# Streams' new states from rows that lie twice, high and low parts in turn, one stream per quarter of 32 rows

## The chip, the cores and the metric

The kernel runs on one core of a Trainium2 chip. The time is the device time of one execution of the whole program, in microseconds (us), and the measure of a kernel is the median of its runs. One further execution was taken with the hardware profiler; its trace gives every instruction's start and end.

## The reference

One layer of a hybrid encoder trunk in float32, for a prompt of 256 frames and for 8 running streams of 16 frames each (384 tokens in all). What matters here is the state space branch (SSD). For each of 8 groups with 8 heads of 64 channels, a new state is computed from the projected and convolved x and B:

```python
step(h, chunk):
    cum = cumsum(dt * A);  xdt = x * dt
    w_end = exp(cum[last] - cum)
    h = h * exp(cum[last]) + einsum('bsgn,bsgr,bsgrp->bgrpn', B, w_end, xdt)
```

The prompt's state starts at zero. Each of the 8 streams starts at its own state and has one chunk of 16 frames, so its new state is the old one decayed plus a sum over its 16 rows of B (128 wide) times the weighted x (64 channels by head). This sum, for 8 streams at once, is what the change rewrites.

## The kernel before

Work is done in stages: early projections and the pooling branch, then the SSD stage (about 420 to 1165 us of the span), then the gate, the output projections and the MLP. TensorE (PE) works through all of them almost without a pause, on products of three: each float32 operand is split into a high part (fp32r) and a low rest, and high times high, high times low and low times high are added up.

A weight block of 128x1024 comes by DMA (`w`), ScalarE (ACT) copies it to its high part (`wh`, line 70) and VectorE (DVE) subtracts for the low part (`wl`, line 71). `take` holds up to three split blocks ahead of PE. A half projection uses one block in 24 matmuls (`half`), and a projection is two halves.

**The SSD stage** loops over 8 groups g. A group has ten projections: x0, B, x1, C, x2, then x3, z0, z1, z2, z3. Two pairs of 128-channel tiles are made of x0..x3: pair 0 (j = 0, 1) and pair 1 (j = 2, 3). Between projections stand two "lumps" of short matmuls: the first after x2, the second after z3. The first lump of a group finishes pair 1 of the group before, the second one pair 0 of the same group. A lump holds t_pp (prompt's state, line 710), in the first lump t_cb (line 666, `cb`), then t_yT and t_Y (lines 688 and 696, `Y`), t_yi (line 675, `py`) and t_su (line 808, `su`). Code written as `lump(...)` is issued in this order on PE.

**t_su** is the sum above. The rows of the streams lie as 128 partitions, 16 for each stream. A matmul contracts 32 rows, a quarter of the array, which are two streams. `Bm` is B times a 0/1 mask that keeps one of the two streams, `xhl` the weighted x in high and low part. For two streams of a quarter, three products and four quarters there are 24 matmuls of 256 columns, into four PSUM tiles `su`. Then DVE adds them to the states (`hs`, line 817).

The pool of PSUM tiles named `ss` has six buffers, given out in turn. In a first lump `cb`, two `Y` and four `su` are seven. So the fourth `su` takes the buffer of `cb`, and its first matmul waits until DVE has read `cb` (`mside`, line 745, which writes `cbm`).

**How x gets its rows.** `turned` makes three steps, run by `tick` at successive half projections: DVE transposes blocks of 32 (`xb`, line 626), POOL issues four DMAs to a DRAM scratch (`t_scr`, line 631), POOL issues one DMA back (line 637), into `xT` (two tiles j of three blocks of 128 rows: two of the prompt, one of the streams) or for B into `Bt`. `xside` (line 761) multiplies by dt for `xdt` and by the weights in place, `hside` (lines 770 and 771) splits into `xhl`, `bside` (lines 723 to 727) splits B and makes `Bm`. All of POOL's DMAs stand in one order on POOL, with its additions of `ssum`.

The order of instructions on each engine is set when the program is built: a scheduler follows the code's order and puts an instruction earlier where it takes its operands to be ready. On the chip each engine runs its own list in that order.

Of the kernel before, what the change touches and what calls it, by code (L numbers as in the profile page):

```python
# [14 lines left out]
P = 128  # L15
T = 384
TP = 256
NB = 8
TS_ = 16
# [3 lines left out]
NH = 64  # L23
# [7 lines left out]
V_GPRE, V_GMLP, V_PSC, V_CW, V_CB, V_NRM, V_DSK, V_DTB, V_ALOG, V_PAR, V_END = 0, 16, 32, 48, 240, 288, 320, 352, 353, 354, 384  # L31


def build(ctx, tc, io):
    nc = tc.nc
    v, s, te, gp, sy = nc.vector, nc.scalar, nc.tensor, nc.gpsimd, nc.sync
# [5 lines left out]
    dram = ctx.enter_context(tc.tile_pool(name="dram", bufs=1, space=DRAM))  # L42
# [3 lines left out]
    vec = consts.tile([P, V_END], F32, name="vec")  # L46
# [6 lines left out]
    def sstile(name):  # L53
        return pss.tile([P, 512], F32, tag="ss", name=name)
# [19 lines left out]
    def dve_later():  # L74
        return behind(cut[1])
# [53 lines left out]
    steps = []  # L129
# [80 lines left out]
    ma_scr = [dram.tile([P, T], F32, name=f"ma_scr{i}") for i in range(KD)]  # L210
    gb_scr = [dram.tile([P, T], F32, name=f"gb_scr{i}") for i in range(KD)]
    t_scr = [dram.tile([T, P], F32, name=f"t_scr{i}") for i in range(40)]
    cum_scr = dram.tile([NH, T], F32, name="cum_scr")
    dec_scr = dram.tile([NH, NB], F32, name="dec_scr")

# [69 lines left out]
    turn, low = [None], [None]  # L285
# [65 lines left out]
    for b in range(3):  # L351
# [3 lines left out]
            out=dgl[:, b, :], in0=ident, scalar=y1, in1=dgh[:, b, :].bitcast(F32), op0=ALU.mult, op1=ALU.subtract  # L355
# [217 lines left out]
    with tc.tile_pool(name="phd", bufs=2, reuse_waits="tile") as pd, tc.tile_pool(  # L573
        name="phd1", bufs=1, reuse_waits="tile"
# [4 lines left out]
        for i in range(3):  # L579
            b = pd1.tile([P, 24, 19], F32, name=f"cbuf{i}")  # L580
# [37 lines left out]
        def conv(ui, c, tag, nb):  # L618
            return taps(conv_in(ui, c), c, tag, nb)

        def turned(src, i, o):
            xb, scr = [], t_scr[i]

            def turn():
                xb.append(pd.tile([P, T], F32, tag="xb", name=f"xb{i}"))
                v.transpose(xb[0], src)

            def spread():
                for q in range(4):
                    p32 = slice(q * 32, q * 32 + 32)  # L630
                    gp.dma_start(
                        scr[:, p32].rearrange("(j a) b -> a j b", a=32),
                        xb[0][p32].rearrange("p (j b) -> p j b", b=32),
                    )

            wait = [lambda: None] if i < 32 else []
            steps.append(wait + [turn, spread, lambda: gp.dma_start(o, scr.rearrange("(b t) n -> t b n", b=3))])

        def xturned(D, g, j):
            S = D.p[j // 2]  # L640
            if j % 2 == 0:
                S.xT = pd.tile([P, 2, 3, P], F32, tag="xT", name=f"xT{S.nm}", bufs=1)
            turned(D.xs[j], g * 4 + j, S.xT[:, j % 2])

        def lump(fn):
            with behind(last[0]):
                last[0] = fn()
# [70 lines left out]
            return i  # L718

        def bside(D):  # L720
            D.Bhl = pd.tile([P, 2, 3, P], F32R, tag="Bhl", name=f"Bhl{D.g}", bufs=1)
            with dve_later():
                s.activation(D.Bhl[:, 0], D.Bt, AF.Copy)
                v.tensor_tensor(D.Bhl[:, 1], D.Bt, D.Bhl[:, 0].bitcast(F32), ALU.subtract)
            D.Bm = pd.tile([P, 2, 2, P], F32R, tag="Bm", name=f"Bm{D.g}", bufs=1)
            for h in range(2):
                s.activation(
                    D.Bm[:, h],
                    D.Bhl[:, :, 2, :].bitcast(F32),
                    AF.Copy,  # L730
                    scale=vec[:, V_PAR + h : V_PAR + h + 1],
                )

        def cside(D):
# [21 lines left out]
        def xside(S):  # L756
            S.xdt = pd.tile([P, 2, 3, P], F32, tag="xdt", name=f"xdt{S.nm}", bufs=1)
            for q in range(2):
                tv = S.xT[:, q].rearrange("p b (h q) -> p b h q", h=2)
                for o, i in ((S.xdt, 3), (S.xT, 6)):  # L760
                    v.tensor_tensor(
                        o[:, q].rearrange("p b (h q) -> p b h q", h=2),
                        tv,
                        tok[:, i : i + 3, S.h0 + q * 2 : S.h0 + q * 2 + 2].unsqueeze(3).to_broadcast([P, 3, 2, 64]),
                        ALU.mult,
                    )

        def hside(S):
            S.xhl = pd.tile([P, 2, 2, 3, P], F32R, tag="xhl", name=f"xhl{S.nm}", bufs=1)
            S.split = s.activation(S.xhl[:, 0], S.xT, AF.Copy)  # L770
            v.tensor_tensor(S.xhl[:, 1], S.xT, S.xhl[:, 0].bitcast(F32), ALU.subtract)

        def eside(S, q):
            if q == 0:
# [26 lines left out]
        def state(S):  # L801
            def t_su():
                su = [sstile(f"su{S.nm}_{q}") for q in range(4)]
                for h in range(2):
                    for n, (bl, xl) in enumerate(((0, 0), (0, 1), (1, 0))):
                        for q in range(4):
                            t = slice(q * 32, q * 32 + 32)
                            i = te.matmul(
                                pairs(su[q][:, h * 256 : h * 256 + 256]),
                                S.D.Bm[t, h, bl, :],  # L810
                                S.xhl[t, xl, :, 2, :].rearrange("p j n -> p n j"),
                                start=n == 0,
                                stop=n == 2,
                            )
                for q in range(4):
                    hr = S.hs[:, 2 * q : 2 * q + 2].rearrange("p h (a n) -> p h a n", a=2)
                    v.tensor_tensor(hr, hr, su[q].rearrange("p (h n a) -> p h a n", h=2, a=2), ALU.add)
                return i

            lump(t_su)  # L820
            gp.dma_start(io["new_ssm_s"][S.qd], S.hs)
# [52 lines left out]
        for g in range(G + 1):  # L874
            if g == G:
                S = prev.p[1]
# [29 lines left out]
            D = Pair()  # L906
# [11 lines left out]
            D.Bt = pd.tile([P, 3, P], F32, tag="Bt", name=f"Bt{g}", bufs=1)  # L918
            turned(D.BT, 32 + g, D.Bt)
# [16 lines left out]
            S = D.p[0]  # L936
# [36 lines left out]
            with nullcontext() if g else behind(S.split):  # L973
                bside(D)
# [24 lines left out]
    with ExitStack() as phe:  # L999
# [21 lines left out]
        for i in range(KD):  # L1021
# [4 lines left out]
            h = mp.tile([P, T], F32R, name=f"mh{i}")  # L1026
            l = mp.tile([P, T], F32R, name=f"ml{i}")
# [42 lines left out]
    with tc.tile_pool(name="phf", bufs=1, side="right", reuse_waits="tile") as pf, tc.tile_pool(  # L1070
        name="phf2", bufs=2, side="right", reuse_waits="tile"
# [79 lines left out]
        for nb in range(4):  # L1151
# [3 lines left out]
            o = [sstile(f"wo{nb}_{b}") for b in range(3)]  # L1155
# [138 lines left out]
        with behind(cd[0]):  # L1294
            for b in range(3):
# [3 lines left out]
                    out=dgl[:, b, :], in0=ident, scalar=y, in1=dgh[:, b, :].bitcast(F32), op0=ALU.mult, op1=ALU.subtract  # L1299
# [12 lines left out]
    with tc.tile_pool(name="phg", bufs=1, reuse_waits="tile") as pg, tc.tile_pool(  # L1312
        name="phg2", bufs=2, reuse_waits="tile"
# [8 lines left out]
        for c8 in range(NC):  # L1322
            hh = []
            for f8 in range(8):
                f = c8 * 8 + f8
                ps = ups[f] if f < 3 else proj([io["w_up"][f, 0], io["w_up"][f, 1]], xs2, f"up{f}")
                t = pg2.tile([P, T], F32, tag="t", name=f"ht{f}")
                for c, w in ((slice(0, TP), slice(0, P)), (slice(TP, T), slice(P, 192))):
                    v.scalar_tensor_tensor(
                        out=halves(t[:, c]), in0=even_odd(ps)[:, :, w], scalar=0.0, in1=halves(r2[:, c]), op0=ALU.max, op1=ALU.mult  # L1330
                    )
                s.activation(t, t, AF.Square)
                h = pg2.tile([P, T], F32R, tag=f"hh{f8}", name=f"hh{f}", bufs=1)
                l = pg2.tile([P, T], F32R, tag=f"hl{f8}", name=f"hl{f}", bufs=1)
# [3 lines left out]
            for nb in range(4):  # L1338
                o = [sstile(f"wd{c8}_{nb}_{b}") for b in range(3)]
# [168 lines left out]
```

## Time and profile before

| | |
|---|---|
| median of 3 runs | 2644.0 us (2642.28 to 2645.38) |
| profiled execution, its own time | 2643.02 us |
| its span, first to last instruction | 2641.2 us |
| around the span | 1.8 us |
| mean granted clock of PE | 0.999 |
| busy: PE, DVE, ACT, POOL | 2629.5, 1545.1, 1162.2, 240.9 us |
| the stretch 594 to 683 us (one group): PE, DVE, ACT, POOL busy | 89.00, 76.30, 56.07, 24.48 us |

A row of a timeline gives the start in us from the span's start, the duration, the engine, the source line, the operation with output and inputs, the shape and how many; in brackets stands how long the engine sat idle before it and what ended that. A duration on PE overlaps the next one, so the spacing of starts tells what a matmul costs; the chain of waits gives these pieces without overlap.

### The profile page before, as it was taken

To read this page: it belongs to the slowest core of one execution; us is meant where nothing else is said; L and a number is where in the kernel's file an instruction comes from. 1 tells how busy PE (TensorE), PEld (TensorE's weight loads), DVE (VectorE), ACT (ScalarE), POOL (GpSimd) and SP (SyncE) were. 2 spreads that over 40 slices of the span, in tenths; PEclk is the share of its full clock that TensorE was granted. 3 is DMA by queue.
4 is the path that set the end of the run, shared out by engine and by line. 5 is a ranking of instruction groups with operands and counts; after the bars stand their busy time and mean duration, and the time that the engine had idled before them with its cause. 6 is when DMAs were issued, how large, how long until landed. Compare 5 with 4: busy or idle time off the path is not lost.

```text
span 2641.2 us, 40719 instructions
## 1 busy us (share of the span) xinstructions
PE 2629.5 (100%) x16317; PEld 2527.7 (96%) x16317; DVE 1545.1 (58%) x2192; ACT 1162.2 (44%) x1781; POOL 240.9 (9%) x382
## 2 busy tenths in 40 slices
PE   9999999999999999999999999999999999999998
PEld 9999999999999999999999989999999999989897
DVE  6685335788888888867444336534444444444446
ACT  6443224656565756545333336433333333323233
POOL 0000002122222322211000000000000000000000
PEclk9999999999999999999999999999999999999999
DMA  7444446666666666657555543444444444444443
GB/s 276 153 132 159 148 145 213 194 203 226 216 228 201 222 219 235 218 190 261 163 166 160 195 149 132 144 136 136 136 136 136 136 136 136 135 135 136 134 135 132
DMA packets 130318, 451.50 MB, mean 171 GB/s; under 512 B 17936, under 2 KB 24912, under 8 KB 125136
## 3 DMA queue, kind: packets, MB, share of 16 engines
q1 hardware_dynamic: 103552, 361.44, 42.3%
q0 software_dynamic: 19520, 72.64, 7.7%
q10 hardware_dynamic: 7056, 14.81, 1.8%
q8 instruction: 128, 2.10, 0.3%
q14 instruction: 62, 0.51, 0.1%
HBM read 404.49 MB, written 44.34 MB: 170 GB/s over the span
## 4 chain that ended last, share of the span: by engine, by line
PE 97%; DMA 1%; DVE 1%; issue 1%; ACT 1%; SPq 0%; DVEq 0%; POOL 0%; ACTq 0%; POOLq 0%
PE pj_up L101 6%; PE pj_up L102 6%; PE pj_up L103 6%; PE wd L156 6%; PE wd L154 6%; PE wd L155 6%; PE pj_x L101 5%; PE pj_x L103 4%; PE pj_x L102 4%; PE pj_sp L103 3%; PE pj_sp L101 3%; PE pj_sp L102 3%; PE pj_z L103 3%; PE pj_z L102 3%; PE pj_z L101 3%; PE pj_gb L101 2%
## 5 line engine op out<-in xcount | busy, mean ns | idle before, releaser
L101 PE MATMUL pj_up<-x1h,wh_up 128*128 128x384 f32 (+1 forms) x1024 | 333.7, 326 | 0.0
L102 PE MATMUL pj_up<-x1l,wh_up 128*128 128x384 f32 (+1 forms) x1024 | 333.4, 326 | 0.0
L103 PE MATMUL pj_up<-x1h,wl_up 128*128 128x384 f32 (+1 forms) x1024 | 333.4, 326 | 0.0
L71 DVE TENSOR_TENSOR wl_wd<-w_wd,wh_wd 128x1024 fp32r<-128x1024 f32 x126 | 154.3, 1225 | 240.3 <-ACT wh_wd L70 240.3
L154 PE MATMUL wd<-wh_wd,hh 128*128 128x512 f32 x756 | 286.5, 379 | 0.0
L155 PE MATMUL wd<-wl_wd,hh 128*128 128x512 f32 x756 | 286.5, 379 | 0.0
L156 PE MATMUL wd<-wh_wd,hl 128*128 128x512 f32 x756 | 286.5, 379 | 0.0
L70 ACT ACTIVATE wh_wd<-w_wd 128x1024 fp32r<-128x1024 f32 x126 | 133.1, 1057 | 321.6 <-PE wd L156 261.2
L70 ACT ACTIVATE wh_up<-w_up 128x1024 fp32r<-128x1024 f32 x126 | 133.1, 1057 | 292.0 <-PE pj_up L102 231.8
L71 DVE TENSOR_TENSOR wl_up<-w_up,wh_up 128x1024 fp32r<-128x1024 f32 x126 | 154.3, 1225 | 178.0 <-ACT wh_up L70 178.0
L101 PE MATMUL pj_x<-xgh,wh_x 128*128 128x384 f32 x768 | 252.0, 328 | 0.3 <-ACT wh_x L70 0.3
L103 PE MATMUL pj_x<-xgh,wl_x 128*128 128x384 f32 x768 | 250.5, 326 | 0.7 <-DVE wl_x L71 0.7
L102 PE MATMUL pj_x<-xgl,wh_x 128*128 128x384 f32 x768 | 250.4, 326 | 0.0
L102 PEld LDWEIGHTS pj_up<-x1l,wh_up 128*128 128x128 f32 x1024 | 193.6, 189 | 0.2
L101 PEld LDWEIGHTS pj_up<-x1h,wh_up 128*128 128x128 f32 x1024 | 193.6, 189 | 0.2
L103 PEld LDWEIGHTS pj_up<-x1h,wl_up 128*128 128x128 f32 x1024 | 193.6, 189 | 0.0
L103 PE MATMUL pj_z<-xgh,wl_z 128*128 128x384 f32 x512 | 167.2, 327 | 0.0
L101 PE MATMUL pj_z<-xgh,wh_z 128*128 128x384 f32 x512 | 166.9, 326 | 0.0
L102 PE MATMUL pj_z<-xgl,wh_z 128*128 128x384 f32 x512 | 166.9, 326 | 0.0
L101 PE MATMUL pj_sp<-abh,wh_sp 128*128 128x384 f32 x512 | 166.9, 326 | 0.0
L102 PE MATMUL pj_sp<-abl,wh_sp 128*128 128x384 f32 x512 | 166.9, 326 | 0.0
L103 PE MATMUL pj_sp<-abh,wl_sp 128*128 128x384 f32 x512 | 166.9, 326 | 0.0
(334 smaller groups left out, 6177.0 us busy)
## 6 DMA issues: line engine op xcount, KB each, us to landing
w_up<-w_up SPq DMA_DIRECT2D x128, 512.0 KB, 3.5
w_wd<-w_down SPq DMA_DIRECT2D x128, 512.0 KB, 3.5
w_x<-w_in SPq DMA_DIRECT2D x96, 512.0 KB, 4.0
w_z<-w_in SPq DMA_DIRECT2D x64, 512.0 KB, 4.4
w_sp<-w_ssd SPq DMA_DIRECT2D x64, 512.0 KB, 3.5
w_ga<-w_ga SPq DMA_DIRECT2D x32, 512.0 KB, 3.5
w_pp<-w_pp SPq DMA_DIRECT2D x32, 512.0 KB, 3.5
hs<-ssm POOLq DMA_DIRECT2D x16, 1024.0 KB, 7.8
```

Of the source, the lines that this page charges most:

```text
L70: cut[0] = s.activation(h, w, AF.Copy)
L71: cut[1] = v.tensor_tensor(l, w, h.bitcast(F32), ALU.subtract)
L101: te.matmul(out, wh, xh, start=first, stop=False, **how)
L102: te.matmul(out, wh, xl, start=False, stop=False, **how)
L103: return te.matmul(out, wl, xh, start=False, stop=last, **how)
L154: te.matmul(out, mh, vh, start=k == 0 and b != held, stop=False, skip_group_check=b == held)
L155: te.matmul(out, mh, vl, start=False, stop=False, skip_group_check=b == held)
L156: last[0] = te.matmul(out, ml, vh, start=False, stop=k == nk - 1, skip_group_check=b == held)
```

## The change

The streams' rows come twice. A new helper `doubled` issues two more DMAs for each tile, one to the even and one to the odd partitions: partitions 2t and 2t+1 both hold row t of the first four streams (l = 0) and of the last four (l = 1). So a quarter of 32 partitions holds one stream of 16 rows, twice, and a second one in the other half of the free dimension. The new tile for x is `xD`, for B `BD`, and the weights come the same way into `tokd`, once, by way of a DRAM scratch `d_scr`. `xT` still gets its three blocks, `Bt` two.

Of the two copies of a row, the even one becomes the negated high part and the odd one the low part of x (`xd`); of B, `Bd` has two parts, high and low, with the sign minus on even and plus on odd partitions. One matmul over 32 rows then adds high times high and high times low, a second one the two products with B's low part. No mask is needed, and t_su has 2 x 2 x 4 = 16 matmuls. `xhl` and `Bhl` lose the streams' block.

```diff
+        def doubled(o, src):
+            for q in range(2):
+                gp.dma_start(o[q::2], src.rearrange("(l t) n -> t l n", l=2))
+
+        tokd = pd.tile([P, 2, NH], F32, name="tokd", bufs=1)
+        gp.dma_start(d_scr, tok[:, 8])
+        doubled(tokd, d_scr)
...
-            steps.append(wait + [turn, spread, lambda: gp.dma_start(o, scr.rearrange("(b t) n -> t b n", b=3))])
+            nb = o.shape[1]
+
+            def fetch():
+                gp.dma_start(o, scr[: nb * P].rearrange("(b t) n -> t b n", b=nb))
+                doubled(od, scr[TP:])
+
+            steps.append(wait + [turn, spread, fetch])
...
         def bside(D):
-            D.Bhl = pd.tile([P, 2, 3, P], F32R, tag="Bhl", name=f"Bhl{D.g}", bufs=1)
+            D.Bhl = pd.tile([P, 2, 2, P], F32R, tag="Bhl", name=f"Bhl{D.g}", bufs=1)
+            D.Bd = pd.tile([P, 2, 2, P], F32R, tag="Bd", name=f"Bd{D.g}", bufs=1)
+            sign = vec[:, V_PAR + 1 : V_PAR + 2]
             with dve_later():
                 s.activation(D.Bhl[:, 0], D.Bt, AF.Copy)
                 v.tensor_tensor(D.Bhl[:, 1], D.Bt, D.Bhl[:, 0].bitcast(F32), ALU.subtract)
-            D.Bm = pd.tile([P, 2, 2, P], F32R, tag="Bm", name=f"Bm{D.g}", bufs=1)
-            for h in range(2):
-                s.activation(
-                    D.Bm[:, h],
-                    D.Bhl[:, :, 2, :].bitcast(F32),
-                    AF.Copy,
-                    scale=vec[:, V_PAR + h : V_PAR + h + 1],
+                s.activation(D.Bd[:, 0], D.BD, AF.Copy, scale=sign)
+                v.scalar_tensor_tensor(
+                    out=D.Bd[:, 1], in0=D.BD, scalar=sign, in1=D.Bd[:, 0].bitcast(F32), op0=ALU.mult, op1=ALU.subtract
                 )
...
+            xD = S.xD.rearrange("p l j (h q) -> p l (j h) q", h=2)
+            v.tensor_tensor(
+                xD, xD, tokd[:, :, S.h0 : S.h0 + 4].unsqueeze(3).to_broadcast([P, 2, 4, 64]), ALU.mult
+            )
 
         def hside(S):
-            S.xhl = pd.tile([P, 2, 2, 3, P], F32R, tag="xhl", name=f"xhl{S.nm}", bufs=1)
-            S.split = s.activation(S.xhl[:, 0], S.xT, AF.Copy)
-            v.tensor_tensor(S.xhl[:, 1], S.xT, S.xhl[:, 0].bitcast(F32), ALU.subtract)
+            S.xhl = pd.tile([P, 2, 2, 2, P], F32R, tag="xhl", name=f"xhl{S.nm}", bufs=1)
+            S.split = s.activation(S.xhl[:, 0], S.xT[:, :, :2], AF.Copy)
+            v.tensor_tensor(S.xhl[:, 1], S.xT[:, :, :2], S.xhl[:, 0].bitcast(F32), ALU.subtract)
+            S.xd = pd.tile([P, 2, 2, P], F32R, tag="xd", name=f"xd{S.nm}", bufs=1)
+            s.activation(S.xd, S.xD, AF.Copy)
+            v.scalar_tensor_tensor(
+                out=S.xd,
+                in0=S.xD,
+                scalar=vec[:, V_PAR : V_PAR + 1],
+                in1=S.xd.bitcast(F32),
+                op0=ALU.mult,
+                op1=ALU.subtract,
+            )
...
-                for h in range(2):
-                    for n, (bl, xl) in enumerate(((0, 0), (0, 1), (1, 0))):
+                for l in range(2):
+                    for part in range(2):
                         for q in range(4):
                             t = slice(q * 32, q * 32 + 32)
                             i = te.matmul(
-                                pairs(su[q][:, h * 256 : h * 256 + 256]),
-                                S.D.Bm[t, h, bl, :],
-                                S.xhl[t, xl, :, 2, :].rearrange("p j n -> p n j"),
-                                start=n == 0,
-                                stop=n == 2,
+                                pairs(su[q][:, l * 256 : l * 256 + 256]),
+                                S.D.Bd[t, part, l],
+                                S.xd[t, l].rearrange("p j n -> p n j"),
+                                start=part == 0,
+                                stop=part == 1,
                             )
```

Where the lists change, it is much the same in every group from the second on. The rows below are of the third group (g = 2), whose first lump has `su` at 637 us of the trace. Numbers in names tell buffers apart: `xT_0` and `xD_0` belong to pair 0, `t_scr_144` and `t_scr_145` to x0 and x1, `t_scr_170` to B, `wl_z_0_0` to the first half of z0.

DVE just ahead of the first lump's readers, before:

```order
L71 TENSOR_TENSOR wl_x_1_6453<-w_x_1_6450,wh_x_1_6452 128x1024
L593 TENSOR_TENSOR cbuf_4139<-pj_x_6415,rstd 128x12x16 x2
L71 TENSOR_TENSOR wl_z_0_0_6603<-w_z_0_0_6600,wh_z_0_0_6602 128x1024
L745 TENSOR_TENSOR cbm_6533<-cb_6493,cst 128x512
L611 TENSOR_SCALAR cacc_6583<-cbuf_4139,vec,cacc_6583 128x384
L832 TENSOR_SCALAR xs_5563<-xs_5563,vec,Y_1_0_6497 128x384
```

and with the change:

```order
L71 TENSOR_TENSOR wl_x_1_6482<-w_x_1_6479,wh_x_1_6481 128x1024
L594 TENSOR_TENSOR cbuf_4140<-pj_x_6444,rstd 128x12x16 x2
L782 TENSOR_TENSOR xD_0_6173<-xD_0_6173,tokd 128x512
L71 TENSOR_TENSOR wl_z_0_0_6631<-w_z_0_0_6628,wh_z_0_0_6630 128x1024
L759 TENSOR_TENSOR cbm_6564<-cb_6524,cst 128x512
L860 TENSOR_SCALAR xs_5581<-xs_5581,vec,Y_1_0_6528 128x384
```

The multiplication of `xD_0` by `tokd`, which waits for the doubled rows of x0 and x1, stands ahead of the split of z0's first block and of the read of `cb`.

POOL's DMAs in the first half of the group, before:

```order
L631 DMA t_scr_144<-xb_6220 32x12x32 x4
L631 DMA t_scr_170<-xb_6283 32x12x32
L637 DMA xT_0_6149<-t_scr_144 128x3x128
L631 DMA t_scr_170<-xb_6283 32x12x32 x3
L637 DMA Bt_6234<-t_scr_170 128x3x128
L631 DMA t_scr_145<-xb_6398 32x12x32 x4
L637 DMA xT_0_6149<-t_scr_145 128x3x128
```

and with the change:

```order
L640 DMA t_scr_144<-xb_6244 32x12x32 x4
L640 DMA t_scr_170<-xb_6308 32x12x32 x2
L649 DMA xT_0_6172<-t_scr_144 128x3x128
L624 DMA xD_0_6173<-t_scr_144 64x2x128 x2
L640 DMA t_scr_170<-xb_6308 32x12x32 x2
L649 DMA Bt_6258<-t_scr_170 128x2x128
L624 DMA BD_6259<-t_scr_170 64x2x128 x2
L640 DMA t_scr_145<-xb_6427 32x12x32 x4
L649 DMA xT_0_6172<-t_scr_145 128x3x128
L624 DMA xD_0_6173<-t_scr_145 64x2x128 x2
```

Each fetch has two issues more behind it: the two for x0 and the two for B stand ahead of x1's way to the scratch, and x1's own two stand behind its `xT`.

DVE at the end of the z projections, before:

```order
L793 TENSOR_TENSOR E_0_6674<-E_0_6674,cbm_6533 128x1024 x2
L964 TENSOR_TENSOR zs_1_6840<-pj_z_1_6774,rstd 128x384
L71 TENSOR_TENSOR wl_z_3_0_6851<-w_z_3_0_6848,wh_z_3_0_6850 128x1024
L71 TENSOR_TENSOR wl_z_3_1_6881<-w_z_3_1_6878,wh_z_3_1_6880 128x1024
L964 TENSOR_TENSOR zs_2_6908<-pj_z_2_6847,rstd 128x384
```

and with the change:

```order
L821 TENSOR_TENSOR E_0_6702<-E_0_6702,cbm_6564 128x1024 x2
L993 TENSOR_TENSOR zs_1_6872<-pj_z_1_6804,rstd 128x384
L71 TENSOR_TENSOR wl_z_3_0_6883<-w_z_3_0_6880,wh_z_3_0_6882 128x1024
L782 TENSOR_TENSOR xD_1_6626<-xD_1_6626,tokd 128x512
L71 TENSOR_TENSOR wl_z_3_1_6913<-w_z_3_1_6910,wh_z_3_1_6912 128x1024
L993 TENSOR_TENSOR zs_2_6940<-pj_z_2_6879,rstd 128x384
```

Here the multiplication of `xD_1`, of x2 and x3, has come ahead of the split of z3's second block. On PE nothing but t_su's matmuls changes; their order with the lump's other parts is the same.

More of the change, by code (lines that the diff above doesn't have):

```diff
@@ L212, in build @@
     t_scr = [dram.tile([T, P], F32, name=f"t_scr{i}") for i in range(40)]
+    d_scr = dram.tile([P, NH], F32, name="d_scr")
     cum_scr = dram.tile([NH, T], F32, name="cum_scr")
@@ L619, in conv, with turned @@
             return taps(conv_in(ui, c), c, tag, nb)
-        def turned(src, i, o):
+        def doubled(o, src):
[4 more added lines that the diff above has]
+        doubled(tokd, d_scr)
+        def turned(src, i, o, od):
             xb, scr = [], t_scr[i]
@@ L642, in xturned @@
                 S.xT = pd.tile([P, 2, 3, P], F32, tag="xT", name=f"xT{S.nm}", bufs=1)
-            turned(D.xs[j], g * 4 + j, S.xT[:, j % 2])
+                S.xD = pd.tile([P, 2, 2, P], F32, tag="xD", name=f"xD{S.nm}", bufs=1)
+            turned(D.xs[j], g * 4 + j, S.xT[:, j % 2], S.xD[:, :, j % 2])
         def lump(fn):
@@ L759, in xside @@
                 tv = S.xT[:, q].rearrange("p b (h q) -> p b h q", h=2)
-                for o, i in ((S.xdt, 3), (S.xT, 6)):
+                for o, i, nb in ((S.xdt, 3, 3), (S.xT, 6, 2)):
                     v.tensor_tensor(
-                        o[:, q].rearrange("p b (h q) -> p b h q", h=2),
-                        tv,
-                        tok[:, i : i + 3, S.h0 + q * 2 : S.h0 + q * 2 + 2].unsqueeze(3).to_broadcast([P, 3, 2, 64]),
+                        o[:, q, :nb].rearrange("p b (h q) -> p b h q", h=2),
+                        tv[:, :nb],
+                        tok[:, i : i + nb, S.h0 + q * 2 : S.h0 + q * 2 + 2].unsqueeze(3).to_broadcast([P, nb, 2, 64]),
                         ALU.mult,
                     )
+            xD = S.xD.rearrange("p l j (h q) -> p l (j h) q", h=2)
+            v.tensor_tensor(
+                xD, xD, tokd[:, :, S.h0 : S.h0 + 4].unsqueeze(3).to_broadcast([P, 2, 4, 64]), ALU.mult
+            )
         def hside(S):
-            S.xhl = pd.tile([P, 2, 2, 3, P], F32R, tag="xhl", name=f"xhl{S.nm}", bufs=1)
-            S.split = s.activation(S.xhl[:, 0], S.xT, AF.Copy)
-            v.tensor_tensor(S.xhl[:, 1], S.xT, S.xhl[:, 0].bitcast(F32), ALU.subtract)
+            S.xhl = pd.tile([P, 2, 2, 2, P], F32R, tag="xhl", name=f"xhl{S.nm}", bufs=1)
[11 more added lines that the diff above has]
+            )
         def eside(S, q):
@@ L808, in t_su @@
                             i = te.matmul(
-                                pairs(su[q][:, h * 256 : h * 256 + 256]),
-                                S.D.Bm[t, h, bl, :],
-                                S.xhl[t, xl, :, 2, :].rearrange("p j n -> p n j"),
-                                start=n == 0,
-                                stop=n == 2,
+                                pairs(su[q][:, l * 256 : l * 256 + 256]),
[3 more added lines that the diff above has]
+                                stop=part == 1,
                             )
                 for q in range(4):
-                    hr = S.hs[:, 2 * q : 2 * q + 2].rearrange("p h (a n) -> p h a n", a=2)
+                    hr = S.hs[:, q::4].rearrange("p h (a n) -> p h a n", a=2)
                     v.tensor_tensor(hr, hr, su[q].rearrange("p (h n a) -> p h a n", h=2, a=2), ALU.add)
@@ L917, in build @@
             D.BT = conv(u0 + 1, 32 + g, "BT", 2)
-            D.Bt = pd.tile([P, 3, P], F32, tag="Bt", name=f"Bt{g}", bufs=1)
-            turned(D.BT, 32 + g, D.Bt)
+            D.Bt = pd.tile([P, 2, P], F32, tag="Bt", name=f"Bt{g}", bufs=1)
+            D.BD = pd.tile([P, 2, P], F32, tag="BD", name=f"BD{g}", bufs=1)
+            turned(D.BT, 32 + g, D.Bt, D.BD)
             if g:
@@ L1446 @@
     vec[:NH, V_ALOG] = a["a_log"][0]
-    for h in range(2):
-        vec[:, V_PAR + h] = (np.arange(P) // TS_) % 2 == h
+    vec[:, V_PAR] = np.arange(P) % 2
+    vec[:, V_PAR + 1] = 2.0 * (np.arange(P) % 2) - 1.0
     d = {
```

## The prediction

> **What bounds the kernel now.** I read the page first, then the chain of waits in the SSD stage, then the timelines of DVE and POOL around the lumps. The page's busy times and its chain:
>
> ```profile
> PE 2629.5 (100%) x16317; PEld 2527.7 (96%) x16317; DVE 1545.1 (58%) x2192; ACT 1162.2 (44%) x1781; POOL 240.9 (9%) x382
> PE 97%; DMA 1%; DVE 1%; issue 1%; ACT 1%; SPq 0%; DVEq 0%; POOL 0%; ACTq 0%; POOLq 0%
> ```
>
> PE has no idle time to win back. A change gains by giving PE less to do and loses by letting it wait. So two questions: how long is a block of t_su, and who stands between PE and its next operand with the new order. First the blocks, from the chain of waits, of the first lumps of groups 1 to 7 (the second to eighth pass of the loop):
>
> ```profile
> 548.64 0.87 PE su L808 x24
> 637.30 0.87 PE su L808 x24
> 726.35 0.87 PE su L808 x24
> 815.00 0.87 PE su L808 x24
> 903.66 0.87 PE su L808 x24
> 992.32 0.87 PE su L808 x24
> 1081.04 0.87 PE su L808 x24
> ```
>
> Every block takes 0.87 us for 24 matmuls, 0.145 us for a set of four quarters. The lumps without cb have the same block; there are 16 in all.
>
> One group's engines, by windows (columns: stretch, length, then busy time of PE, PEld, DVE, ACT, POOL, clock, DMA share, GB/s):
>
> ```profile
> 594.00:683.00 89.00, 89.00 (x682) 86.23 (x681) 76.30 (x112) 56.07 (x104) 24.48 (x36) 1.00 0.66 217
> ```
>
> DVE is the second busiest, with 12.7 us free in 89, ACT has 33.
>
> **The change part by part.**
>
> *t_su itself.* 24 matmuls become 16, four sets instead of six: 2 x 0.145 = 0.29 us less by block, 16 blocks: **-4.6 us**. Nothing hides it, PE is the path. It is also all that can be won: 0.18% of the time. I take the share as proportional; if part of the 0.87 us is fixed, less is won. The Trainium skill, "TensorE: Matmul & The Clock Gate", Part 3 (packing small matmuls), gives four row tiles one matmul's duration plus about 4 ns for each further tile; for 256 columns at its 2.4 GHz I estimate 0.119 us by set, and the gain would be 3.8 us. The trace's 0.145 us by set is a little longer, and decides.
>
> *DVE's and ACT's work.* Every pair gives DVE two operations of 512 (`xD`, `xd`), every group one of 256 (`Bd`); its others get shorter. Nearest durations:
>
> ```profile
> L771 DVE TENSOR_TENSOR xhl<-xT,xhl x16: 944/952/960, 468.3 to 1137.3; 128x768 fp32r<-128x768 f32 x16
> L770 ACT ACTIVATE xhl<-xT x16: 825/843/856, 467.1 to 1136.2; 128x768 fp32r<-128x768 f32 x16
> 636.34 0.68 DVE L745 TENSOR_TENSOR cbm<-cb,cst 128x512 f32<-128x512 f32 x1
> ```
>
> At 0.68 us for 512 that is at most 4 x 0.68 + 0.68 = 3.4 us by group, without what gets shorter; 12.7 us are free. ACT gets a copy of 512 by pair, under 0.84 us, and loses one mask copy by group; 33 us are free. As mere work both cost nothing: PE's cover is `take`'s three blocks of lead. Without it PE would wait for a `wl`. `tokd` is fetched once, in the first group, beside PE's projections: nothing.
>
> *POOL's issues and the wait that is added.* This is the costly part. In a first lump the fourth `su` waits for `cbm`, since it takes the buffer of `cb`. DVE's rows of group 2 before:
>
> ```profile
> 634.68 0.62 DVE L593 TENSOR_TENSOR cbuf<-pj_x,rstd 128x192 f32<-128x192 f32 x2
> 635.21 1.22 DVE L71 TENSOR_TENSOR wl_z<-w_z,wh_z 128x1024 fp32r<-128x1024 f32 x1
> ```
>
> with `cbm` (above) from 636.34 to 637.02, and `su` at 637.30. Only 0.3 us lie between. With the change `xD_0` stands ahead of this `wl_z`. It waits for the last of x1's three fetches, and `wl_z` and `cbm` are queued behind it, PE behind `cbm`. When does that fetch land? POOL's rows for x1 in groups 1 to 7, way out and way back:
>
> ```profile
> 537.33 2.45 POOL L631 DMA_DIRECT2D t_scr<-xb  x4 [1.23 <-DVE xb L626]
> 543.45 0.76 POOL L637 DMA_DIRECT2D xT<-t_scr  x1 [3.66 <-DMA t_scr<-xb]
> 627.61 2.45 POOL L631 DMA_DIRECT2D t_scr<-xb  x4 [1.58 <-DVE xb L626]
> 633.86 0.75 POOL L637 DMA_DIRECT2D xT<-t_scr  x1 [3.80 <-DMA t_scr<-xb]
> 714.69 2.45 POOL L631 DMA_DIRECT2D t_scr<-xb  x4 [2.50 <-DVE xb L626]
> 719.20 0.75 POOL L637 DMA_DIRECT2D xT<-t_scr  x1 [2.06 <-DMA t_scr<-xb]
> 804.79 2.45 POOL L631 DMA_DIRECT2D t_scr<-xb  x4 [2.77 <-DVE xb L626]
> 809.39 0.75 POOL L637 DMA_DIRECT2D xT<-t_scr  x1 [2.14 <-DMA t_scr<-xb]
> 893.01 2.46 POOL L631 DMA_DIRECT2D t_scr<-xb  x4 [2.29 <-DVE xb L626]
> 898.15 0.75 POOL L637 DMA_DIRECT2D xT<-t_scr  x1 [2.67 <-DMA t_scr<-xb]
> 982.30 2.45 POOL L631 DMA_DIRECT2D t_scr<-xb  x4 [2.34 <-DVE xb L626]
> 986.91 0.75 POOL L637 DMA_DIRECT2D xT<-t_scr  x1 [2.16 <-DMA t_scr<-xb]
> 1071.00 2.45 POOL L631 DMA_DIRECT2D t_scr<-xb  x4 [1.61 <-DVE xb L626]
> 1079.24 0.75 POOL L637 DMA_DIRECT2D xT<-t_scr  x1 [5.78 <-DMA t_scr<-xb]
> ```
>
> and the landings, counted from the start of the issue: of the `xT` at 543.45, at 809.39 and at 1079.24, of all `xT`, of all that touches the scratch:
>
> ```profile
> DMA to landing us min/median/max: 2.7/2.7/2.7
> DMA to landing us min/median/max: 4.2/4.2/4.2
> DMA to landing us min/median/max: 4.6/4.6/4.6
> DMA to landing us min/median/max: 2.7/3.8/8.3
> DMA to landing us min/median/max: 2.0/3.5/8.3
> ```
>
> From the start of that `xT`: its issue 0.75, the even half's issue 0.62 (an issue of t_scr: 2.45 / 4 = 0.61), then the odd half's landing. No row shows this DMA (64 partitions, 64 KB). Bounds are 2.0 us (the fastest of the scratch) and 4.6; I take 2.7, what the `xT` with the same source took in its quiet cases. So the rows lie there 4.07 us after `xT`'s start. Then DVE's three in a row, each started 0.08 us before the other's end as above: `xD` 0.61, `wl_z` 1.13, `cbm` 0.68, together 2.42. The fourth `su` can start 6.49 us after `xT`, and without a wait would start 0.11 us (three matmuls) after the block's start. So PE waits 6.38 us less the distance from `xT` to `su`.
>
> That distance is 5.19, 3.44, 7.15, 5.61, 5.51, 5.41 and 1.80 us in groups 1 to 7. Besides, x1's way out comes later where POOL has no room: four issues are new ahead of it (2.48 us), and its idle time there (the brackets) takes up 1.23, 1.58, 2.50, 2.77, 2.29, 2.34 and 1.61 of it. What is left, 1.25, 0.90, 0, 0, 0.19, 0.14 and 0.87, adds to the wait. By group: 6.38 - 5.19 + 1.25 = 2.4; 3.8; nothing (short by 0.8); 0.8; 1.1; 1.1; 5.5: **+14.7 us**. Where an `xT` landed late, at 809 and 1079, its doubled rows come right behind it and I give them the same delay, 1.5 and 1.9 us: **+3.4 us**. Group 0 has no `su` in its first lump, and the last pass has no cb.
>
> By the Trainium skill, "DMA: Bandwidth & Descriptors", Anatomy of one DMA (gpsimd path), a DMA takes 2.0 us plus its bytes over 436 KB per us; for 64 KB I estimate 2.15 us, and six waits would be 0.55 us shorter, 3.3 us in all. The trace is slower than that rule for `xT`: 2.45 us by it, 2.7 at the least and 3.8 in the median.
>
> *The second new wait.* `xD_1` stands ahead of the `wl_z` of z3's second block:
>
> ```profile
> 666.92 0.75 POOL L637 DMA_DIRECT2D xT<-t_scr  x1 [3.57 <-DMA t_scr<-xb]
> 667.53 1.21 DVE L71 TENSOR_TENSOR wl_z<-w_z,wh_z 128x1024 fp32r<-128x1024 f32 x1
> 669.15 1.23 DVE L71 TENSOR_TENSOR wl_z<-w_z,wh_z 128x1024 fp32r<-128x1024 f32 x1 [0.41 <-ACT wh_z L70]
> 678.08 0.67 PE py L710 x6
> L103 PE MATMUL pj_z<-xgh,wl_z 128*128 128x384 f32 x512 | 167.2, 327 | 0.0
> ```
>
> The rows land at 666.92 + 4.07 = 671.0, DVE is there at 668.7, so it waits 2.3 us, and with `xD`'s 0.61 `wl_z` ends 2.9 us later, at 673.3. PE's matmuls of 327 ns follow each other two deep, 0.163 us apart; z3's second half ends where the lump starts, and its third matmul is the first with `wl_z`: 678.08 - 24 x 0.163 + 0.33 = 674.5. It is in time, by 1.2 us; nothing is counted. Cover gone, it would cost what the landing takes beyond that.
>
> **The sum:** -4.6 + 14.7 + 3.4 = +13.5 us on the profiled execution's own 2643.0 us, 2656.5. The median of the runs is 1.0 us above that execution, well inside their spread of 3 us; I say **2656.5 us**. With the landing at 2.0 in the six groups and none late, the waits are 14.7 - 6 x 0.7 = 10.5 and the time 2649; with 3.8 us, the median, in all seven, 14.7 + 6 x 1.1 + 0.3 = 21.6 and 2660, and with x1's way out 1 us slower as well, since it now follows B's fetches without a pause, 2667. That is the forecast's own range.
>
> **The rivals.**
>
> *The rows are there in time.* If POOL's path is faster than in this trace, `xD_0` finds its rows, `cbm` is on time, and only the saving is left: 2643.0 - 4.6 = 2638.4 us, not slower. For it: in group 3 the distance of 7.15 us already does that. It needs 6.4 us from `xT` to `su` in all groups, and six of seven have less; the shortest landings of 2.0 us don't suffice for groups 1, 2 and 7. Small waits up to the bound of a measurable change belong here.
>
> *Landings as slow as the slowest x1.* If the doubled fetches crowd the queue and each lands in 4.6 us, the first lumps wait 14.7 + 6 x 1.9 + 1.1 = 27.2 us and the second wait comes through: 4.6 - 2.7 - 1.2 = 0.7 us in each of 8 groups, 5.6 us. 2643.0 - 4.6 + 27.2 + 5.6 = 2671 us. For it: two of seven did land so late. Against: the other five took 2.7 or 2.8.
>
> *The block doesn't shrink,* since something fixed sets its 0.87 us: 4.6 us more than forecast, 2661. Against it: the projections' rows show no fixed part, 24 matmuls take 24 spacings, and `su`'s seven pieces are alike.
>
> **How the numbers follow.** About 0.2% (5.3 us) is what a measurement of this kernel can tell from no change. Forecast 0.56; rows in time 0.24, of which 0.03 would be faster than 0.2% (the block falling by more than its share); slow landings 0.15; block unchanged 0.05. Faster 0.03, same 0.22 (in-time cases beside it, with 0.01 of the forecast's lowest), slower 0.75. To hold 8 in 10 the range reaches down to the rival in time, 2638.4, and up to the slow landings, 2671. As signs differ, the forecast's own range is 2649 to 2667.
>
> **What would show it.** In the profile of the changed kernel: blocks of `su` with 16 matmuls and 0.58 us in the second lumps; in the first lumps of groups 1 to 7 PE idle before `su`, released by DVE `cbm`, 0 to 6 us each and some 15 to 18 in all; DVE idle before `xD`, put down to a DMA from the scratch, twice a group; no PE wait for the last `wl_z`; POOL's new issues at 0.5 to 0.75 us. The prediction is wrong if PE has no idle time in front of `cbm`'s reader, or if PE waits elsewhere, for a `wl` or `wh`.

## The result and the profile after

The changed kernel is slower: 2667.7 us, median of 6 runs (2664.39 to 2669.25), against 2643.4 of the kernel before on the same chip (6 runs, 2642.19 to 2645.38). The ratio is 1.0087, 95% interval 1.0076 to 1.0097. The forecast was 2656.5 us in a range of 2638.4 to 2671: sign and range held, but the loss is 24.4 us instead of 13.1 over that median. The profiled execution took 2668.8 us with a span of 2666.9, 25.7 us more than before; the mean granted clock is 0.996 instead of 0.999.

The page's busy times and the chain of the changed kernel:

```profile
PE 2638.1 (99%) x16189; PEld 2534.7 (95%) x16189; DVE 1549.0 (58%) x2232; ACT 1162.2 (44%) x1789; POOL 288.3 (11%) x465
PE 58%; DVE 3%; DMA 2%; ACT 1%; issue 1%; POOL 1%; SPq 0%; DVEq 0%; POOLq 0%; ACTq 0%
```

PE has 128 matmuls less and yet is busy 8.6 us longer: some of its matmuls have become slower. And it no longer holds the chain alone. (The chain is followed back to 901 us only, so its shares add up to two thirds of the span.) The waits of 400 to 1250 us (engine, line, for whom, sum, times, longest):

```profile
PE su L836 <- DVE cbm L759: 14.9, 6, 4.3
PE pj_x L103 <- DVE wl_x L71: 2.4, 4, 0.7
DVE xD L782 <- DMA xD<-t_scr: 43.4, 12, 5.8
DVE xD L782 <- issue: 7.6, 2, 4.0
```

This is the predicted wait: DVE stands in front of `xD` for its rows twice a group, and PE behind `cbm` in six of the first lumps. The chain in group 5, where PE alone stood before (pieces left out between):

```profile
908.86 3.62 DMA t_scr<-xb
...
914.24 0.76 POOL xT L649
914.99 0.61 POOL xD L624
915.61 4.54 DMA xD<-t_scr
...
920.94 1.22 DVE wl_z L71
922.16 0.60 DVE cbm L759
```

x1's way out, the issues, the landing of the odd half, DVE. The same place in the timelines of DVE and PE (start, duration, and in brackets the idle time before):

```profile
920.33 0.69 DVE L782 TENSOR_TENSOR xD<-xD,tokd 128x512 f32<-128x512 f32 x1 [5.80 <-DMA xD<-t_scr]
920.94 1.22 DVE L71 TENSOR_TENSOR wl_z<-w_z,wh_z 128x1024 fp32r<-128x1024 f32 x1
922.08 0.68 DVE L759 TENSOR_TENSOR cbm<-cb,cst 128x512 f32<-128x512 f32 x1
```

```profile
918.12 0.38 PE L836 MATMUL su<-xd,Bd 32*128 32x256 f32 x3
922.81 1.22 PE L836 MATMUL su<-xd,Bd 32*128 32x256 f32 x13 [4.32 <-DVE cbm L759]
923.96 0.69 PE L101 MATMUL pj_x<-xgh,wh_x 128*128 128x384 f32 x1
924.44 0.53 PE L102 MATMUL pj_x<-xgl,wh_x 128*128 128x384 f32 x1
929.27 0.33 PE L101 MATMUL pj_x<-xgh,wh_x 128*128 128x384 f32 x1
```

Read them across: the odd half's fetch starts at 915.61, `xD` starts at 920.33, `cbm` 1.75 us later, and the fourth `su` 2.48 us after `xD`'s start. Then something that the prediction does not have: the 13 matmuls take 1.22 us (0.71 in group 7, where the clock stayed at 1.00), and the projection's matmuls 0.53 us each instead of 0.33, until 928.6. The windows around that place (stretch, length, busy times, and third from the end the granted clock):

```profile
915.00:921.80 6.80, 3.49 (x71) 2.28 (x70) 1.47 (x2) 1.74 (x5) 1.21 (x2) 1.00 0.36 128
921.80:928.63 6.83, 5.82 (x28) 5.59 (x29) 6.83 (x12) 3.81 (x12) 2.00 (x2) 0.50 0.27 96
928.63:935.00 6.37, 6.37 (x41) 6.37 (x40) 6.30 (x13) 6.04 (x12) 2.69 (x5) 1.00 0.59 219
```

PE runs at half clock for 6.83 us, from during the wait to well behind it. Windows of half a microsecond over the whole stage find three such stretches: 734.07 to 740.90, 829.64 to 833.06 and this one; before there is none. The sum over the three:

```profile
sum 17.08, PE 14.49 PEld 14.05 DVE 17.08 ACT 9.88 POOL 5.39; mean PE 4.83 PEld 4.68 DVE 5.69 ACT 3.29 POOL 1.80
```

PE is busy for 14.49 us in them, work of 7.2 us at full clock: 7.2 us lost.

So the 25.7 us are: -3.5 for the blocks (below), +14.9 of waits for `cbm`, +7.2 of half clock, +2.7 of PE's other waits (4.1 instead of 1.4 us in this stage, the largest `wl_x`). That is 21.3. Of the 4.4 left, some 2.2 belong to the waits as well: a first matmul behind a gap doesn't overlap its predecessors. In group 2 the fourth matmul of the block starts 642.35 - 640.07 = 2.28 us after the first, of which 1.91 are idle and 0.01 is the usual distance in a block without a wait; 0.36 us are lost besides, and six times that is 2.2. The rest lies ahead of the first block of `su`, before any such wait: that block starts at 507.47 us instead of 503.96, and only 1.2 of these 3.5 us are waits counted above. In the traces of the ten experiments it starts between 502.2 and 506.7 us, also where the kernel before is the base (502.2 to 505.5), so this part can be spread between executions; that the change causes it isn't shown.

### The profile page after: what moved, and what is told of

Its sections match the earlier page's. It is cut to its first block, busy times and chain, and to the rows that moved or that the text cites. A ratio compares the mean times of both kernels' runs of the same rounds, so it can differ in the third digit from the quotient of the medians.

```text
span 2666.9 us, 40636 instructions
## 1 busy us (share of the span) xinstructions
PE 2638.1 (99%) x16189; PEld 2534.7 (95%) x16189; DVE 1549.0 (58%) x2232; ACT 1162.2 (44%) x1789; POOL 288.3 (11%) x465
## 4 chain that ended last, share of the span: by engine, by line
PE 58%; DVE 3%; DMA 2%; ACT 1%; issue 1%; POOL 1%; SPq 0%; DVEq 0%; POOLq 0%; ACTq 0%
PE pj_up L101 6%; PE pj_up L103 6%; PE pj_up L102 6%; PE wd L156 6%; PE wd L155 6%; PE wd L154 6%; PE pj_sp L103 3%; PE pj_sp L102 3%; PE pj_sp L101 3%; PE pj_gb L101 2%; PE pj_gb L103 2%; PE pj_gb L102 2%; PE wo L156 2%; PE wo L155 2%; PE wo L154 2%; DMA t_scr<-xb 1%
```

## The experiments

**Both `xD` moved, `cbm` and the weights ahead.** `behind` keeps an instruction behind another one in the list; `cut[1]` is the last `wl` issued so far. Theory: the loss is a landing that is passed on. Rival: the new DMAs or DVE's longer list cost the time.

```diff
-            v.tensor_tensor(D.cbm, D.cb, cst[:, C_MASK : C_MASK + 512], ALU.mult)
+            D.read = v.tensor_tensor(D.cbm, D.cb, cst[:, C_MASK : C_MASK + 512], ALU.mult)
...
-            v.tensor_tensor(
-                xD, xD, tokd[:, :, S.h0 : S.h0 + 4].unsqueeze(3).to_broadcast([P, 2, 4, 64]), ALU.mult
-            )
+            with behind(S.D.read if S.jp == 0 else cut[1]):
+                v.tensor_tensor(
+                    xD, xD, tokd[:, :, S.h0 : S.h0 + 4].unsqueeze(3).to_broadcast([P, 2, 4, 64]), ALU.mult
+                )
```

> The changed kernel, but pair 0's xD multiplication stands behind cbm on DVE and pair 1's behind a weight block two halves on, so nobody who feeds PE is queued behind a landing. Theory: the loss is the wait for the landing, passed on by cbm to su, and what that wait does to PE's clock. Then PE has no idle time in front of su, the clock is 1.00 through the SSD stage, and 16 blocks of 0.65 us instead of 0.87 us are left: 2643.4 - 3.5 = 2639.9 us, up to 2642 if the small waits for wl remain. Rival (the 64 new DMAs on POOL's queue or DVE's longer list cost the time by themselves): the time stays above 2655 us.

Measured: 2639.4 us (11 runs; before 2644.0), ratio 0.9982 (0.9974 to 0.9991). That is faster than both kernels. The same place in group 2, DVE and PE:

```profile
635.76 1.23 DVE L71 TENSOR_TENSOR wl_z<-w_z,wh_z 128x1024 fp32r<-128x1024 f32 x1 [0.31 <-ACT wh_z L70]
636.90 0.68 DVE L759 TENSOR_TENSOR cbm<-cb,cst 128x512 f32<-128x512 f32 x1
646.21 0.68 DVE L783 TENSOR_TENSOR xD<-xD,tokd 128x512 f32<-128x512 f32 x1
639.27 0.72 PE L837 MATMUL su<-xd,Bd 32*128 32x256 f32 x16
```

`cbm` ends 1.7 us ahead of `su`; `xD` starts 9.3 us after `cbm` does and finds its rows there. All DMAs and all work are as in the change; only their place on DVE differs. The rival falls: nearly the whole loss hung on that place.

**The place without the landing.** The same order on DVE ahead of `cbm`, but the multiplication there reads constants (the streams' x is left out of the sum). `xmul` issues it behind `cin[0]`, the last `cbuf`. Pair 1's multiplication reads constants too, but stands behind a weight block, as in the experiment above.

```diff
...
-                xD, xD, tokd[:, :, S.h0 : S.h0 + 4].unsqueeze(3).to_broadcast([P, 2, 4, 64]), ALU.mult
...
+                    xE,
+                    cst[:, C_MASK : C_MASK + 512].rearrange("p (l h q) -> p l h q", l=2, h=4),
+                    tokd[:, :, S.h0 : S.h0 + 4].unsqueeze(3).to_broadcast([P, 2, 4, 64]),
+                    ALU.mult,
...
+            with behind(xmul(S, cin[0])):
+                mside(D)
```

> The changed kernel with the same order on DVE: in place of xD's multiplication, at the same place ahead of wl_z_0_0 and cbm, a multiplication of the same size of constants, which waits for no DMA (the streams' x is left out of the sum; all fetches are still made). Theory (landing): only the work of 0.7 us is ahead of cbm, 0.3 us of which is covered; PE waits 0.3 to 0.5 us in seven lumps, about 3 us, too short for the clock: 2643.4 - 3.5 + 3 = 2643 us. Rival (the place in the list or the work costs, not the landing): waits of 2 us and more in front of su remain, and the time is above 2655 us.

Measured: 2639.5 us, ratio 0.9984 (0.9975 to 0.9993). DVE in group 2, with `su` at 635.42:

```profile
631.52 0.68 DVE L786 TENSOR_TENSOR xE<-cst,tokd 128x512 f32<-128x512 f32 x1
632.12 1.22 DVE L71 TENSOR_TENSOR wl_z<-w_z,wh_z 128x1024 fp32r<-128x1024 f32 x1
633.26 0.68 DVE L759 TENSOR_TENSOR cbm<-cb,cst 128x512 f32<-128x512 f32 x1
```

No PE wait at all, so even the 3 us that I still allowed for the work were too many: `cbm` ends 1.5 us before `su`. So the wait comes from the landing, not from the operation or its place as such.

**The saving by itself.** The kernel before without the third of its three products (so it leaves low B times high x out).

```diff
-                    for n, (bl, xl) in enumerate(((0, 0), (0, 1), (1, 0))):
+                    for n, (bl, xl) in enumerate(((0, 0), (0, 1))):
```

> The kernel before with the third product of t_su left out (high times high and high times low only), so 16 matmuls a block as in the changed kernel and nothing else changed. It measures the term of the saving by itself. The prediction's step: 0.29 us a block, 16 blocks, 4.6 us: 2643.4 - 4.6 = 2638.8 us. From the changed kernel's trace (16 matmuls start to start in 0.65 us against 0.87): 0.22 us a block, 3.5 us, 2639.9 us. Rival (a block has a fixed part that hides the smaller number): no change, 2643.4 us. The pieces of the chain tell the first two apart, the time only the third.

Measured: 2638.3 us (before 2643.2), ratio 0.9981 (0.9972 to 0.9990). The first two of its chain's 16 pieces, all of them 0.65 us:

```profile
502.28 0.65 PE su L808 x16
546.66 0.65 PE su L808 x16
```

So a set of four quarters more or less is (0.87 - 0.65) / 2 = 0.11 us, and by this 0.21 us of a block is fixed: 0.22 us a block, 3.5 us in all. (In the changed kernel too, a block of a second lump without a wait takes 0.65 us; 0.58 was forecast.) The interval of the times (2.6 to 7.4 us) holds this and my 4.6; the pieces decide.

**The fetches by themselves.** The kernel before with the doubled fetches, into tiles that nobody reads. (There are 80 new issues, 8 groups of five tiles and two each; the 144 of the expectation was miscounted.)

```diff
...
+                doubled(od, scr[TP:])
...
```

> The kernel before with all doubled fetches of x and B added, into tiles that nobody reads: the 144 new issues on POOL's queue and their traffic, without a wait on DVE. Theory: the queue has room and the weights are not disturbed, so no PE wait and 2643 to 2645 us. Rival (the DMAs by themselves hold up the way of the rows or the weights): PE waits for operands in each group, 2650 us and more.

Measured: 2642.8 us, ratio 0.9999 (0.9990 to 1.0008). Three of its first lumps have blocks 0.06 to 0.31 us longer, no more. Landings of 2.3 to 7.8 us, median 3.9, as slow as in the change, cost nothing that the times show when no one in PE's path waits for them.

**PE's waits by themselves.** In the kernel before, work ahead of `cbm` and no new DMA. First `cbm`'s multiplication made twice, and four times with 4 for the 2:

```diff
-            v.tensor_tensor(D.cbm, D.cb, cst[:, C_MASK : C_MASK + 512], ALU.mult)
+            for _ in range(2):
+                v.tensor_tensor(D.cbm, D.cb, cst[:, C_MASK : C_MASK + 512], ALU.mult)
```

> The kernel before, with cbm's multiplication made twice: the second ends some 1.1 us later, so su waits about 0.8 us in seven lumps. Theory: 6 us of waits and no half clock, since the waits are short: 2643 + 6 = 2649 us. Rival (any stop of PE halves its clock for some us): 1.5 us and more besides in each lump, 2660 us and above.

> The kernel before, with cbm's multiplication made four times; other work of DVE falls between them, so the last ends some 3.5 us later by the durations of the list. No new DMA, no xD. Theory (a wait of PE of some 3 us costs itself and, after it, half clock for a while): seven waits of about 3.2 us, 22 us, and 1 to 3 us of half clock behind most of them, 14 us: 2643 + 36 = 2679 us, with the granted clock at 0.50 behind some su. Rival (waits cost only themselves, the half clock comes from something else in the change): clock 1.00 and 2665 us.

Measured: twice 2646.7 us (ratio 1.0010, 1.0001 to 1.0019), four times 2649.3 (1.0022, 1.0013 to 1.0032). PE's waits for `su`, of the one and of the other:

```profile
PE su L809 <- DVE cbm L746: 3.0, 4, 1.1
```

```profile
PE su L809 <- DVE xs L833: 3.1, 3, 1.6
```

The first agrees with the theory in kind, not in size: there is no half clock, but there are four waits of 0.19 to 1.09 us instead of seven of 0.8, and 2.7 us instead of 6. The second missed its aim: `su` waited for `xs`, the reader of a `Y`, not for the last `cbm`, so with this order it seems to have had another buffer, and seven waits of 3.2 us became three of 0.42, 1.04 and 1.59. Still, the longest of them had half clock behind it, from 909.93 to 913.34. Then longer delays, with multiplications of 128x2048 ahead of `cbm`, two and three:

```diff
-            mside(D)
...
+            f = cin[0]
+            for _ in range(2 if g else 0):
+                with behind(f):
+                    f = v.tensor_tensor(
+                        fill, cst[:, :1].to_broadcast([P, 2048]), cst[:, :1].to_broadcast([P, 2048]), ALU.mult
+                    )
+            with behind(f):
+                mside(D)
```

> The kernel before with two multiplications of 128x2048 on DVE (about 2.3 us each by hs's row) put ahead of cbm in groups 1 to 7; no new DMA. With one other operation between them cbm ends some 4 us later: su waits about 3.7 us in seven lumps, 26 us. Theory (PE's clock falls to half behind such a wait, and comes back on a grid of some 3.4 us): half clock behind most of the seven, each costing 1.7 to 3.4 us, 14 us in all: 2643.4 + 26 + 14 = 2683 us. Rival (the wait costs only itself; the half clock of the changed kernel has another cause, such as DMA traffic or the new matmuls): clock 1.00 and 2669 us.

> As with two multiplications, but three, and one more operation between: su waits about 6.3 us in seven lumps, 44 us. Theory: every wait now covers a whole stretch of the grid, so the clock is at half behind all seven, 2.5 us each on top, 17 us: 2705 us. Rival (waits cost only themselves): 2687 us and clock 1.00.

Measured: two 2676.8 us (ratio 1.0128, 1.0114 to 1.0142), three 2700.8 (1.0219, 1.0203 to 1.0234). The waits and one lump of each (rows of the timeline and a window):

```profile
PE su L808 <- DVE cbm L745: 16.5, 7, 3.3
642.36 1.64 PE L808 MATMUL su<-xhl,Bm 32*128 32x256 f32 x11 [2.05 <-DVE cbm L745]
644.42 0.53 PE L102 MATMUL pj_x<-xgl,wh_x 128*128 128x384 f32 x1
642.14:648.97 6.83, 6.61 (x27) 6.38 (x28) 6.68 (x14) 6.15 (x11) 0.74 (x2) 0.50 0.46 154
```

```profile
PE su L808 <- DVE cbm L745: 33.4, 7, 5.6
650.59 1.62 PE L808 MATMUL su<-xhl,Bm 32*128 32x256 f32 x6 [5.44 <-DVE cbm L745]
647.29:657.53 10.24, 6.94 (x23) 6.74 (x24) 10.23 (x15) 7.07 (x13) 2.89 (x3) 0.50 0.39 155
```

The waits came out shorter than expected (16.5 and 33.4 us instead of 26 and 44). In the two rows 13 and 18 of the block's 24 matmuls run ahead of the wait (11 and 6 are left), where it was 3 in the change; how much of the difference this explains was not measured. The times lie 33.6 and 57.6 us above before, 17 and 24 us more than the waits. Six of the seven lumps with two, all seven with three have half clock behind them; the sums over these stretches, found as above, of the one and of the other:

```profile
sum 34.14, PE 32.06 PEld 31.04 DVE 33.52 ACT 30.02 POOL 3.21; mean PE 5.34 PEld 5.17 DVE 5.59 ACT 5.00 POOL 0.54
```

```profile
sum 54.63, PE 41.41 PEld 40.06 DVE 54.56 ACT 41.50 POOL 13.26; mean PE 5.92 PEld 5.72 DVE 7.79 ACT 5.93 POOL 1.89
```

Half of PE's busy time in them is 16.0 and 20.7 us. With the waits that makes 32.5 of 33.6 and 54.1 of 57.6 us. Waits alone would give 2660 and 2677 us, so the rival falls: waits of PE halve its clock without any new DMA or new matmul.

**The path of the rows.** The changed kernel without B's doubled fetches (B's part in the streams' sum takes other rows), so x1 goes out with two issues fewer ahead.

```diff
-                doubled(od, scr[TP:])
+                if i < 32:
+                    doubled(od, scr[TP:])
...
-            D.BD = pd.tile([P, 2, P], F32, tag="BD", name=f"BD{g}", bufs=1)
+            D.BD = D.Bt
```

> The changed kernel without the two doubled fetches of B in each group (B's part takes prompt rows in their stead, so the streams' sum is over other values). Two issues of 0.61 us fewer stand ahead of x1's way out on POOL; the order on DVE is the same. Prediction's term (x1's way out is later by what POOL has no room for): x1's rows are back up to 1.2 us earlier in groups 2 to 7, the waits in front of su fall from 15 us to 8 to 10 us and one or two of the three stretches of half clock go: 2655 to 2660 us. Rival (the landing alone sets the wait, POOL's place does not matter): waits and time as with the change, 2665 to 2669 us.

Measured: 2664.5 us, ratio 1.0080 (1.0064 to 1.0095), waits and landings:

```profile
PE su L837 <- DVE cbm L760: 11.5, 4, 4.7
DMA to landing us min/median/max: 2.2/3.7/6.6
```

The waits lie between the two, four instead of six and 11.5 us instead of 14.9, but there are still three stretches of half clock, and the interval of the time doesn't tell it from that of the change, as the rival had it. So it isn't shown that POOL's place matters. From `xT`'s issue to `su` it is 5.6 us on average, against 5.1 with the change; but it is 5.6 as well in the kernel with both `xD` moved, which makes all the fetches. The landings stay as they were.

**The second wait by itself.** Only pair 0's `xD` moved, pair 1's ahead of `wl_z` as in the change. The edit against the kernel with both moved:

```diff
-            with behind(S.D.read if S.jp == 0 else cut[1]):
+            with behind(S.D.read) if S.jp == 0 else nullcontext():
```

> As in the kernel with both multiplications moved, but only pair 0's xD stands behind cbm; pair 1's xD stays ahead of wl_z of z3's second block, as in the change. It measures the second wait by itself. The prediction's step: DVE waits there in every group, PE does not, 0 us, so the same 2639.4 us as with both moved. Rival (the wait is carried on, since DVE's list is full behind it, to the wl_x of the next groups, where the changed kernel showed PE waits of 0.5 us): 1 to 3 us more, 2641 to 2642 us, with PE waits for wl_x in the trace.

Measured: 2640.9 us, ratio 0.9989 (0.9980 to 0.9998), with both moved 0.9982 (0.9974 to 0.9991): not to be told apart. DVE waits there, and no wait of PE follows from it (PE's waits for `wl_x` are 1.5 us in this stage, 1.3 with both moved):

```profile
DVE xD L783 <- DMA xD<-t_scr: 17.4, 5, 4.5
DVE xD L783 <- issue: 7.9, 2, 4.0
```

## Why the prediction was right in sign and too small

**The new wait: right in place, in kind and in sum.** PE idles before the fourth `su`, released by `cbm`, `xD` waiting twice a group. The sum was 14.7 + 3.4 = 18.1 us, the trace has 14.9. By group it was not right (us; distance is from `xT`'s issue to `su`, rows is from `xT`'s issue to `xD`'s start on DVE):

| group | 1 | 2 | 3 | 4 | 5 | 6 | 7 |
|---|---|---|---|---|---|---|---|
| wait predicted, late landings in it | 2.4 | 3.8 | 0 | 2.3 | 1.1 | 1.1 | 7.4 |
| wait measured | 0 | 1.91 | 3.88 | 1.49 | 4.32 | 0.52 | 2.83 |
| distance | 7.87 | 5.77 | 2.70 | 4.56 | 3.88 | 6.90 | 4.28 |
| rows | 3.97 | 5.57 | 4.47 | 3.95 | 6.09 | 5.32 | 5.00 |

The step from the rows to `su` held: 2.48 us in group 5, 2.42 in the prediction. The two other terms were read off single rows of before and were both off. The rows took 4.9 us on average instead of 4.07, since the landings (of all 64 fetches of `xD`) are 3.8 us in the median and not 2.7; and the distances were 5.1 us on average, where mine less the later way out come to 30.8 / 7 = 4.4. The one made the waits longer, the other shorter. (Before, the distances are 4.9 us on average, so the later way out that I added, 3.4 us in all, isn't to be seen in these traces.) That the sum came out is partly luck; that there is a wait of 0 to 5 us in most groups was not.

**The step that failed: a wait of PE was priced at its length.** The prediction had no term for PE's clock. Half clock took 7.2 us here, and 16 and 21 us in the two kernels with longer delays. With it the sum, 18.1 + 7.2 - 4.6 = 20.7 us, comes near the 24.4 measured. Besides, a wait costs some 0.36 us more than PE's idle time, since the matmul behind it no longer overlaps those ahead. The rival of slow landings, 2671 us, came near the time by longer waits, which were not there.

**The saving: right mechanism, too large.** I took 24 to 16 matmuls as proportional, 0.29 us a block. It is 0.22 us, 3.5 us in all: the mean of a set holds a fixed part. The Trainium skill, "TensorE: Matmul & The Clock Gate", Part 3 (packing small matmuls), from which I had estimated 0.119 us a set, is close to the measured 0.11 and was the better price for a set more or less; my sentence that the trace's 0.145 decides compared a mean with a marginal cost.

**Counted at nothing and right:** the fetches' traffic and POOL's issues (0.9999 by themselves), the second wait (not to be told from none), DVE's and ACT's work (no wait when only the work stood there). One sign that the prediction had named against itself, a wait of PE for a `wl`, is in the trace, but small: 2.4 us for `wl_x`, of which 1.3 come before 445 us, where the kernel before has 0.7. Why the other two came, of 0.5 us each, stays open.

**The way on.** The idea of the change wins 4.6 us (2.4 to 6.9 by the interval; the blocks alone give 3.5), if the multiplication that needs the rows stands behind the one that frees PE's buffer. That is the kernel with both `xD` moved.

## What to carry to other kernels

An engine's list is a queue for those behind: before an operation that waits for a DMA, look what stands next in the list and who waits for that, and put the operation that feeds the bottleneck first. In these traces a wait of a TensorE that is otherwise hardly ever idle costs its length, and from 1.24 us on it was mostly followed by 3.4 to 10 us at half clock as well. What a smaller count saves is read from the difference of two counts, not from the mean.

## What the hardware showed

In the SSD stage half clock came only in stretches of 3.41, 6.83 or 10.24 us, once, twice and three times 3.413. (Every trace, that of before too, also ends at half clock, which begins after PE's last matmul.) Within a run they start on one grid: in the changed kernel at 734.07, 829.64 and 921.80, 28 and 27 times 3.413 us apart. The Trainium skill, "TensorE: Matmul & The Clock Gate", Part 1 (the clock gate), says that the clock follows a free-running window of 3.41 us, and the traces agree to the hundredth. Its section "Why this matters for your kernels" asks for no idle gap over some 3 us; here shorter ones did it too. All waits of 3.0 us and more were followed by half clock, none up to 1.09 us, and between these it was not a matter of length: 1.24, 1.49, 1.59, 2.05 and 2.74 us were, 1.91 and 2.83 us were not. The grid alone doesn't sort them either. The 1.24 us lay within one window, and half clock followed; of the 1.91 and 2.83 us, 1.46 and 1.74 lay in one window, with the rest in the next, and none did. So what decides, besides the idle time in a window, stays open.
